# Moving the first head pair's value products behind six more projection steps, and halving the first four loads over two queues

## The chip, the cores and the metric

The kernel runs on one core of a Trainium2 chip. A core has five engines that run their own instruction streams and meet at semaphores: TensorE (PE in the profile; PEld is its weight load), VectorE (DVE), ScalarE (ACT), GpSimd (POOL) and SyncE (SP). SP, ACT and POOL can issue DMA transfers. The metric is the device time of one execution in microseconds, lower is better; times are given as the median of several runs.

## The reference

Two layers of a hybrid encoder over 512 new prompt frames and 8 running streams of 16 frames, 640 frames in all, width 1024, in float32. Cut to what matters here:

```python
x = x + 0.5 * swiglu(rmsnorm(x, g1), w_gu, w_down)          # first feed-forward half step
z = rmsnorm(x, gm) @ w_in                                    # conv B, C, V | q, k, v | gates
s = (q @ k.T) * 64 ** -0.5 + rel_bias[clipped distance]      # 8 heads of 64
s = where(valid chunk band, s, -1e30)
y_attn = softmax(s) @ v
m = sigmoid(g_c) * (y_conv @ w_conv_out) + sigmoid(g_a) * (y_attn @ w_attn_out)
x = x + m @ w_o
x = x + 0.5 * swiglu(rmsnorm(x, g2), w_gu2, w_down2)         # second half step
```

New keys, values and convolution states are outputs too. The first half step begins with the frames `x` and the first weights of `w_gu` in HBM. For the part of the change in the mixer, what counts is that `softmax(s) @ v` of one pair of heads and the projections of the next pairs do not depend on each other.

## The kernel before

**Products.** Every large product is made of three passes of a reduced float32 type: an operand is cut by ACT into `hi` (a cast, line 370) and by DVE into `lo` (the rest, line 376), and PE adds hi·hi, hi·lo and lo·hi in PSUM. Weights come as slabs of 128x1024 from one stream in HBM, cut two slabs ahead of their use. The products of attention itself (scores, transposes, values) are plain float32.

**The opening** (lines 476 to 499 and `opening`, 764 on). Line 479 loads the first half of the frames of `x[0]` with the gains of the first norm (`head`) from SP, line 481 the first 256 columns of weight slab 0 (`raws[0]`) from ACT, line 482 the other half of `x[0]` from SP. The loop at 494 then issues, all from SP, for k = 1 to 7 the block `x[k]` (line 496, 320 KB) and 256 columns of slab 0 or 1 (line 498, 128 KB); line 499 loads the small parameters. `opening` issues a small ACT copy (768, the first ACT work, which loads the activation table), 16 idle products on PE (777), and then for each k the cut of the frames (`plain`, lines 669 to 688), the cut of the weights (`piece`, 785 and 786) and, after each odd k, the 24 products of blocks k-1 and k with both slabs (line 800 for the first 12 of them, 446 for all others). Call blocks 0 and 1 with their weights couple 0, blocks 2 and 3 couple 1.

**The mixer.** In `attention` the order of PE's instructions is the order of the program; ACT, DVE and POOL are ordered by the framework's planner, in which `with soon()` raises a group's priority. A projection of two column tiles (`seven`) is a scheme of seven block products instead of eight. It is cut into 14 steps of six products of 128x320, and `fill(n)` runs the next n steps of the stream of projections. The 14 steps, two at a time, use three PSUM banks: `pa` on X11, `pb` on X21, `pa` on N6, `pc` on T5, `pa` on T7, `pc` on X22, `pa` on T4. Each two are followed by work that reads the bank: the ACT copies of `pa` (line 891), `pa` (899) and `pc` (903), and the DVE additions `first`, `second`, `third` and `last`. A bank is added to further after it was read: the X22 products go on in `pc` after the copy of 903, and the T4 products go on in `pa` after the addition `second` (line 299, `k<-ma_qk,c` in the profile).

For one pair of heads p, `scores(p)` (line 1950) makes the score products into four `att` and two `pr` banks, DVE adds bias and takes maxima (1956), ACT does the exponentials (2150); `turn` transposes the weights on PE (1987) and copies them to SBUF; `values(p)` (2019) makes 16 products into one `att` bank `py`, and ACT copies it to `yas` (2022). Lines 2028 to 2035 give the order for pair 0: `fill(4)`, `turn(0, 0)`, `fill(2)`, `turn(0, 1)`, `fill(2)`, `values(0)`, `fill(6)`, `scores(2)`; for later pairs `values(p)` stands right ahead of `scores(p + 2)`. The six steps behind `values(0)` are, counted from the profile, step 12 (the second X22 step) and steps 13 and 14 (T4) of the projection of q and k of pair 2, and then steps 1 to 3 of that of pair 3. This order is run once in each of the two layers.

Of the kernel before, what the change touches and what calls it, by code (L numbers as in the profile page):

```python
# [16 lines left out]
P = 128  # L17
HP = P // 2
# [5 lines left out]
T = SEQ + NB * TS  # L24
HT = T // 2
# [6 lines left out]
KT = D // P  # L32
# [27 lines left out]
PAD = 64  # L60
# [136 lines left out]
def trunk(ctx: ExitStack, tc: tile.TileContext, xin, wst, small, pbias, samplebias, kcache, vcache, gfin,  # L197
          yout, yrows, ko, vo, co):
    nc = tc.nc
    PE, DVE, ACT, POOL, SP = nc.tensor, nc.vector, nc.scalar, nc.gpsimd, nc.sync  # L200
# [59 lines left out]
    raws, ready = [], []  # L260
# [215 lines left out]
    x = [xp.tile([P, T if k else KT + T], F32, name=f"x{k}") for k in range(KT)]  # L476
    head = x[0][:, :KT]
    m = KT + HT
    SP.dma_start(x[0][:, :m], xin[:, PAD - KT : PAD + HT])
    raws += [wp.tile([P, CH], F32, tag="raw", name=f"raw{i}", bufs=3) for i in range(2)]  # L480
    ACT.dma_start(raws[0][:, : 2 * P], wst[0][:, : 2 * P])
    SP.dma_start(x[0][:, m:], xin[:, PAD + HT : PAD + T])
    x[0] = x[0][:, KT:]
    ident = cp.tile([P, P], F32, name="ident")
    make_identity(nc, ident)
# [7 lines left out]

    for k in range(KT):
        if k:
            SP.dma_start(x[k], xin[:, PAD + k * T : PAD + (k + 1) * T])
            c = slice(k // 2 * 2 * P, (k // 2 + 1) * 2 * P)
            SP.dma_start(raws[k % 2][:, c], wst[k % 2][:, c])
    SP.dma_start(sm, small)
# [903 lines left out]
    def mixer(l, after):  # L1403
        with tc.tile_pool(name=f"yp{l}", bufs=1, reuse_waits="tile") as yp, \
# [18 lines left out]
            with tc.tile_pool(name=f"mp{l}", bufs=2, reuse_waits="tile") as mp:  # L1423
# [62 lines left out]
                with tc.manual_schedule(engines={mybir.EngineType.PE}):  # L1486
                    attention(l, h, st, stats, ops, mp, yas, ycp, both, others())
# [362 lines left out]
    def attention(l, h, norms, stats, ops, mp, yas, ycp, both, others):  # L1850
# [36 lines left out]
        def fill(n):  # L1887
            for _ in range(n):
                next(stream, None)
# [85 lines left out]
        def turn(p, first=None):  # L1975

            if p not in turned:
                turned[p] = [mp.tile([P, offs[-1] + SEQ], F32, name=f"pt{l}_{2 * p + e}", tag="pt")
                             for e in range(2)]
            pt = turned[p]  # L1980

            def blocks(ps, e, js):
                s = weights[2 * p + e]
                n = 0
                for j in js:
                    for i in range(j, NQ):
                        PE.transpose(ps[:, n : n + P], s[:, offs[i] + j * P : offs[i] + (j + 1) * P], ident)
                        n += P

            def take(copy, e, js, ps):  # L1990
                n = sum(width[j] for j in js)
                with soon():
                    copy(pt[e][:, at[js[0]] : at[js[0]] + n], ps[:, :n])

            parts = ((0,), (DVE.tensor_copy,) * 2), ((1, 3), (DVE.tensor_copy, ACT.copy))
            if first is not None:
                parts = (((3, 2), (DVE.tensor_copy, ACT.copy)),) if first else (
                    parts[0], ((1,), (ACT.copy, DVE.tensor_copy)))
            for js, copies in parts:
                for e in range(2):  # L2000
                    ps = (pr if first and not e else att)(f"ptp{l}_{2 * p + e}_{js[0]}")
                    blocks(ps, e, js)
                    take(copies[e], e, js, ps)
            if first is not None:
                return
            ps = pr(f"ptp{l}_{2 * p}_2")
            for e in range(2):
                blocks(ps[:, e * width[2] :], e, (2,))
            for e in range(2):
                take(DVE.tensor_copy, e, (2,), ps[:, e * width[2] :])  # L2010

        def values(p):

            pt = turned.pop(p)
            py = att(f"py{l}_{p}")
            for j in range(NQ):
                for e in range(2):
                    hh = 2 * p + e
                    PE.matmul(py[e * HD : (e + 1) * HD, j * P :], vs[j][:, hh * HD : (hh + 1) * HD],
                              pt[e][:, at[j] : at[j] + width[j]], start=j == 0, stop=j == NQ - 1)  # L2020
            with soon():
                ACT.copy(yas[:, p, 0:SEQ], py)
# [6 lines left out]
        turn(0, 0)  # L2029
        fill(2)  # L2030
        turn(0, 1)
        fill(2)
        values(0)
        fill(6)
        scores(2)
        for p in range(1, npair):
            if p + 1 < npair:
# [487 lines left out]
```

## Time and profile before

| what | us |
|---|---|
| median of 3 runs (lowest to highest) | 2466.82 (2466.36 to 2468.04) |
| the profiled execution's own time | 2465.41 |
| its span, first to last instruction | 2463.6 |
| HBM read over the span | 241.58 MB at a mean of 101 GB/s with what is written |

The page's first part gives each engine's busy time, its share of the span and its instructions; POOL is busy 328.7 us, 13%. In its second part the span stands in 40 slices; the granted TensorE clock is in its highest tenth in all of them. The timeline view gives one line for each instruction or run of like instructions: start in us from the span's start, duration in us, engine (a q behind its name is its sequencer, which issues or waits), line, operation, tiles written and read, shape and count, and in brackets how long the engine was idle before and what ended that. Products on PE overlap, so their pitch is the distance of two starts and not the duration.

### The profile page before, as it was taken

The page shows a single profiled execution, that of the slowest core. Times are in us where ns is not written, and L with a number is a line of the kernel's source. Part 1 is how long each engine was busy: PE and PEld are TensorE (multiplying, and loading weights), DVE is VectorE, ACT ScalarE, POOL GpSimd, SP SyncE. Part 2 cuts the span into 40 slices and gives each one's busy share as a digit, 9 for nine tenths or more (in the row PEclk, how much of TensorE's full clock was granted, in tenths as well). Part 3 has the DMA queues.
Part 4 walks back from the last instruction along what each step waited for, and adds up shares of the span by engine and source line. Part 5 has one row for each costly group of instructions (what it writes and reads, how often), then busy time and mean ns, then how long its engine had stood idle before and what let it go on. Part 6 is the DMA issues. An engine that isn't in the chain of part 4 may idle for free.

```text
span 2463.6 us, 44155 instructions
## 1 busy us (share of the span) xinstructions
PE 2457.2 (100%) x17238; PEld 2409.1 (98%) x17238; DVE 2196.6 (89%) x3729; ACT 1397.6 (57%) x2252; POOL 328.7 (13%) x495
## 2 busy tenths in 40 slices
PE   9999999999999999999999999999999999999999
PEld 9999999889999999999999999998899999999998
DVE  7999999888998899998799999988889989999997
ACT  6555556665655555555665555566656555555555
POOL 0211112211110001011001111121110000111111
PEclk9999999999999999999999999999999999999999
DMA  4543445335443234444334343452444433444444
GB/s 156 143 123 103 117 118 127 112 107 176 119 129 122 87 102 113 108 118 123 107 98 109 109 120 99 118 129 101 140 163 118 123 116 94 108 113 107 113 119 118
DMA packets 115282, 290.93 MB, mean 118 GB/s; under 512 B 13088, under 2 KB 53664, under 8 KB 115072
## 3 DMA queue, kind: packets, MB, share of 16 engines
q1 hardware_dynamic: 69984, 219.96, 26.7%
q0 software_dynamic: 44800, 67.75, 14.6%
q8 instruction: 135, 2.21, 0.4%
q14 instruction: 75, 0.61, 0.1%
q10 hardware_dynamic: 288, 0.39, 0.0%
HBM read 241.58 MB, written 7.94 MB: 101 GB/s over the span
## 4 chain that ended last, share of the span: by engine, by line
PE 100%; ACT 0%; DVE 0%; issue 0%; DVEq 0%; POOL 0%; POOLq 0%
PE pab L470 13%; PE paa L470 11%; PE pcb L470 6%; PE pca L470 6%; PE daa L1204 6%; PE dab L1204 5%; PE po L446 5%; PE qa L470 4%; PE pbb L470 3%; PE pba L470 3%; PE dca L1204 3%; PE dcb L1204 3%; PE ma_cv L470 2%; PE ma_qk L470 2%; PE pv L1903 2%; PE poa L446 2%
## 5 line engine op out<-in xcount | busy, mean ns | idle before, releaser
L370 ACT CAST whi<-raw 128x1024 fp32r<-128x1024 f32 (+1 forms) x564 | 500.5, 892 | 375.8 <-DVE raw L299 63.9
L376 DVE TENSOR_TENSOR wlo<-raw,whi 128x1024 fp32r<-128x1024 f32 (+1 forms) x602 | 580.0, 966 | 136.2 <-ACT whi L370 132.7
L370 ACT CAST whi<-s 128x1024 fp32r<-128x1024 f32 (+1 forms) x166 | 155.3, 935 | 283.4 <-issue 111.2
L470 PE MATMUL pab<-xhib,whi 128*128 128x320 f32 x704 | 217.5, 309 | 0.0
L470 PE MATMUL pab<-xhib,wlo 128*128 128x320 f32 x704 | 217.1, 308 | 0.0
L470 PE MATMUL pab<-xlob,whi 128*128 128x320 f32 x704 | 217.1, 308 | 0.0
L470 PE MATMUL paa<-xhia,wlo 128*128 128x320 f32 x640 | 197.8, 309 | 0.0
L470 PE MATMUL paa<-xhia,whi 128*128 128x320 f32 x640 | 197.7, 309 | 0.0
L470 PE MATMUL paa<-xloa,whi 128*128 128x320 f32 x640 | 197.4, 309 | 0.0
L376 DVE TENSOR_TENSOR wlo<-s,whi 128x1024 fp32r<-128x1024 f32 (+1 forms) x169 | 179.1, 1060 | 3.8 <-ACT whi L370 3.8
L1226 POOL DMA_DIRECT2D x<-c_a x80 | 70.0, 1019 | 569.2 <-ACT ahia L1105 244.8
L1226 POOL DMA_DIRECT2D x<-c_b x72 | 63.0, 1006 | 582.0 <-ACT ahib L1105 205.8
L470 PEld LDWEIGHTS pab<-xhib,whi 128*128 128x128 f32 x704 | 132.2, 188 | 0.9 <-issue 0.9
L470 PEld LDWEIGHTS pab<-xlob,whi 128*128 128x128 f32 x704 | 132.2, 188 | 0.0
L470 PEld LDWEIGHTS pab<-xhib,wlo 128*128 128x128 f32 x704 | 132.1, 188 | 0.0
L470 PEld LDWEIGHTS paa<-xhia,wlo 128*128 128x128 f32 x640 | 120.1, 188 | 0.5 <-DVE wlo L376 0.4
L470 PEld LDWEIGHTS paa<-xhia,whi 128*128 128x128 f32 x640 | 120.1, 188 | 0.5 <-issue 0.4
L470 PEld LDWEIGHTS paa<-xloa,whi 128*128 128x128 f32 x640 | 120.1, 188 | 0.0
L299 DVE TENSOR_TENSOR raw<-s,raw 128x512 f32<-128x512 f32 x166 | 113.1, 682 | 0.0
L470 PE MATMUL pcb<-xhib,wlo 128*128 128x320 f32 x352 | 108.5, 308 | 0.0
L470 PE MATMUL pcb<-xhib,whi 128*128 128x320 f32 x352 | 108.5, 308 | 0.0
L470 PE MATMUL pcb<-xlob,whi 128*128 128x320 f32 x352 | 108.5, 308 | 0.0
(922 smaller groups left out, 8249.1 us busy)
## 6 DMA issues: line engine op xcount, KB each, us to landing
raw<-in_wst SPq DMA_DIRECT2D x374, 512.0 KB, 3.6
x<-c_a POOLq DMA_DIRECT2D x80, 160.0 KB, 4.5
x<-c_b POOLq DMA_DIRECT2D x72, 160.0 KB, 3.6
one<-in_wst POOLq DMA_DIRECT2D x40, 256.0 KB, 3.8
lent<-in_wst POOLq DMA_DIRECT2D x36, 256.0 KB, 4.0
kc<-in_kcache SPq DMA_DIRECT2D x32, 256.0 KB, 4.7
vc<-in_vcache SPq DMA_DIRECT2D x16, 512.0 KB, 4.4
x<-u_a POOLq DMA_DIRECT2D x40, 160.0 KB, 4.3
```

The source lines that it names most:

```text
L299: DVE.tensor_tensor(out=out, in0=a, in1=b, op=op)
L370: ACT.copy(hi[:, d], src[:, c])
L376: DVE.tensor_tensor(out=lo, in0=src, in1=hi.bitcast(F32), op=ALU.subtract)
L446: PE.matmul(ps[:, a, :HT], w, x[a] if isinstance(x, tuple) else x[:, a * HT : (a + 1) * HT], start=first and j == 0 and not seeded, stop=l ...
L470: PE.matmul(ps, a, b, start=start and kp == 0 and j == 0, stop=stop and kp == NP - 1 and j == 2, skip_group_check=True)
L1204: PE.matmul(ps[u], w, y, start=start and i == 0 and j == 0, stop=i == 1 and j == 2, skip_group_check=True)
L1226: POOL.dma_start(x[ms[2 * u + r]][:, cols], z[:, u], accum_op=ALU.add)
L1903: PE.matmul(pv[t], xx[:, t * P : (t + 1) * P], w[:, kk * AW : (kk + 1) * AW], start=c == 0 and kk == 0 and j == 0, stop=c == KT // 2 - 1 a ...
```

## The change

The four first loads (both halves of `x[0]`, the first part of slab 0, and `x[1]`) are each issued as two transfers of 64 partitions, the lower from SP and the upper from ACT. The later loads stay whole and on SP. In `attention`, in both layers, `values(0)` moves from behind the second of eight projection steps to behind all eight, right ahead of `scores(2)`.

```diff
@@ -476,10 +476,16 @@
     head = x[0][:, :KT]
     m = KT + HT
-    SP.dma_start(x[0][:, :m], xin[:, PAD - KT : PAD + HT])
+    def sent(out, src):
+        for q, c in ((SP, slice(0, HP)), (ACT, slice(HP, P))):
+            q.dma_start(out[c], src[c])
+
+    sent(x[0][:, :m], xin[:, PAD - KT : PAD + HT])
     raws += [wp.tile([P, CH], F32, tag="raw", name=f"raw{i}", bufs=3) for i in range(2)]
-    ACT.dma_start(raws[0][:, : 2 * P], wst[0][:, : 2 * P])
-    SP.dma_start(x[0][:, m:], xin[:, PAD + HT : PAD + T])
+    sent(raws[0][:, : 2 * P], wst[0][:, : 2 * P])
+    sent(x[0][:, m:], xin[:, PAD + HT : PAD + T])
...
     for k in range(KT):
         if k:
-            SP.dma_start(x[k], xin[:, PAD + k * T : PAD + (k + 1) * T])
+            (sent if k == 1 else SP.dma_start)(x[k], xin[:, PAD + k * T : PAD + (k + 1) * T])
             c = slice(k // 2 * 2 * P, (k // 2 + 1) * 2 * P)
             SP.dma_start(raws[k % 2][:, c], wst[k % 2][:, c])
@@ -2029,9 +2035,8 @@
         turn(0, 0)
         fill(2)
         turn(0, 1)
-        fill(2)
+        fill(8)
         values(0)
-        fill(6)
         scores(2)
```

## The prediction, made before the changed kernel was timed

> **What bounds the kernel now.** I read the page first, then PE's waits, then the timeline of the two places that the change touches.
>
> ```profile
> span 2463.6 us, 44155 instructions
> PE 2457.2 (100%) x17238; PEld 2409.1 (98%) x17238; DVE 2196.6 (89%) x3729; ACT 1397.6 (57%) x2252; POOL 328.7 (13%) x495
> PE 100%; ACT 0%; DVE 0%; issue 0%; DVEq 0%; POOL 0%; POOLq 0%
> ```
>
> The last line is the chain of work that ended last: it is PE from end to end. PE is busy 2457.2 of 2463.6 us, so its idle time is worth at most 6.4 us, and the whole of PE's listed waiting is this:
>
> ```profile
> PE idle L777 <- POOL epst L491: 1.1, 1, 1.1
> ```
>
> So an edit gains only if PE starts useful products earlier, or spends less time changing from one kind of product to another; it loses as soon as PE has to wait. Both places are looked at with starts, since a busy PE also hides short waits. These are the rows of the opening:
>
> ```profile
> 0.74 0.41 ACTq L481 DMA_DIRECT2D raw<-in_wst  x1
> 0.74 0.39 SPq L479 DMA_DIRECT2D x<-in_xin  x1
> 1.18 1.28 ACT L768 ACT_TABLE_LOAD   x1 [1.18 <-PEq L2497]
> 1.65 0.43 SPq L496 DMA_DIRECT2D x<-in_xin  x1
> 2.12 0.43 SPq L498 DMA_DIRECT2D raw<-in_wst  x1
> 2.47 0.19 ACT L768 COPY early<-epst 128x1 f32<-128x1 f32 x1
> 2.60 0.43 SPq L496 DMA_DIRECT2D x<-in_xin  x1
> 3.92 0.56 ACT L688 ACTIVATE xhia<-x 128x320 fp32r<-128x320 f32 x1 [1.26 <-DMA x<-in_xin]
> 4.39 0.39 ACT L785 CAST whi<-raw 128x256 fp32r<-128x256 f32 x1
> 4.83 0.41 PE L800 MATMUL poa<-xhia,whi 128*128 128x320 f32 x1
> ...
> 7.14 0.33 SPq L496 DMA_DIRECT2D x<-in_xin  x1
> 7.15 0.56 ACT L688 ACTIVATE xhia<-x,x 128x320 fp32r<-128x320 f32 x1 [0.58 <-DMA x<-in_xin]
> 8.36 0.33 SPq L496 DMA_DIRECT2D x<-in_xin  x1
> 8.37 0.83 ACT L675 ACTIVATE xhia<-x,x 128x640 fp32r<-128x640 f32 x1
> 9.23 0.88 DVE L669 SCALAR_TENSOR_TENSOR xloa<-x,x,xhia 128x640 fp32r<-128x640 f32 x1
> 10.17 0.30 PEld L446 LDWEIGHTS poa<-xloa,whi 128*128 128x128 f32 x2 [0.15 <-DVE xloa L669]
> ```
>
> The first real product starts at 4.83, 0.91 after the first operand landed (3.92). From then on PE waits for data once more that counts, 0.15 at 10.17, and the chain to there is the landing of x[2] at 7.15, ACT's cuts up to 9.20, DVE's cut of x[3] from 9.23 to 10.11. Whatever starts PE earlier than 4.83 is waited for again at 10.17, and a later start is free up to about those 0.15 us.
>
> **The change, part one: the halved loads.** Four more transfers are issued: ahead of the first load of slab 1 SP has four (before three), ACT four (before one).
>
> ```profile
> L2068 SPq DMA_DIRECT2D vn<-v x8: 512/518/607, 526.0 to 608.1; - x8
> ```
>
> This is the only transfer of few partitions here, 16 of them, and its issue takes 0.518 us, more than the 0.43 of a whole x load. So a half costs a whole issue: I take 0.47 from the starts 1.65, 2.12, 2.60. ACT then issues at 0.74, 1.18, 1.65 and 2.12 and is free at 2.55 instead of 1.15; its table load (1.28) ends at 3.86 where it ended at 2.46, the small copy (0.19) at about 4.05, and as ACT begins an operation some 0.09 ahead of the end of the one before (3.92 + 0.56 against 4.39), the first cut starts at 3.97 at the earliest, against 3.92. The 1.26 us of idle time ahead of it are the cover, and they are used up. Whether the halves of x[0] land earlier than 3.92 is then of no use. First product: 4.83 + 0.05 = 4.88, inside the 0.15 that PE waits at 10.17 anyway. I count 0.
>
> The other cost is in SP's later issues. Counted in order of issue (slab 0 from ACT, two halves of x[0], x[1], then weights and x in turn), the 6th load is x[2], the 8th x[3], the 14th x[6] and the 16th x[7]. The 14th (7.14) goes out as the 6th lands (ACT takes it at 7.15), the 16th (8.36) as the 8th lands (8.37). So a load waits for the one eight places ahead of it. With four extra transfers, the ninth is now the second slab's first part (2.12 before), and it waits for the first half of x[0]: some 3.5 to 3.9. Everything behind it on SP moves back by the same 1.4 to 1.8 us: x[2] from 2.60 to 4.0 to 4.4. What hides this is the queue's backlog: x[2] lands 4.55 after its issue (2.60 to 7.15), where the first load with nothing ahead of it takes 3.18 (0.74 to 3.92), and the bytes ahead of it stay the same. If the transfers are never starved, x[2] lands at about 7.15 again: 0. With the 3.18 of the unloaded load it would land at 7.2 to 7.6. If nothing of the shift were hidden, PE would wait up to 1.8 longer at 10.17. Ends: -0.5 (x[2] lands earlier by nearly the 0.58 that ACT is idle ahead of it) and +1.8. I take 0: 7.2 is nearest to the row of 7.15, and the 0.15 at 10.17 is there for the rest.
>
> [...]
>
> **Part two: values(0) behind the six steps.** The rows of layer 0, then three of layer 1:
>
> ```profile
> 492.69 0.41 ACT L903 COPY c<-mc_qk 128x320 f32<-128x320 f32 x1
> 492.97 0.31 PE L470 MATMUL ma_qk<-thi,wlo 128*128 128x320 f32 x1
> 492.99 1.06 ACT L370 CAST whi<-raw 128x1024 fp32r<-128x1024 f32 x1
> 493.15 0.41 PE L470 MATMUL mc_qk<-hhim,whi 128*128 128x320 f32 x1
> 493.41 0.31 PE L470 MATMUL mc_qk<-hlom,whi 128*128 128x320 f32 x1
> 493.99 0.31 PE L470 MATMUL mc_qk<-hhim,wlo 128*128 128x320 f32 x1
> 494.08 1.23 DVE L376 TENSOR_TENSOR wlo<-raw,whi 128x1024 fp32r<-128x1024 f32 x1 [1.42 <-ACT whi L370]
> 494.23 2.37 PE L2019 MATMUL py<-pt,v 128*64 128x512 f32 x16
> 495.22 0.48 DVE L299 TENSOR_TENSOR k<-ma_qk,c 128x320 f32<-128x320 f32 x1
> 496.54 0.41 PE L470 MATMUL mc_qk<-hhim,whi 128*128 128x320 f32 x1
> 496.79 0.31 PE L470 MATMUL mc_qk<-hlom,whi 128*128 128x320 f32 x1
> 497.52 0.31 PE L470 MATMUL ma_qk<-thi,whi 128*128 128x320 f32 x1
> 502.01 2.43 PE L1950 MATMUL pss<-k,q 64*128 64x512 f32 x16
> ...
> 1716.06 0.31 PE L470 MATMUL mc_qk<-hhim,wlo 128*128 128x320 f32 x1
> 1717.29 0.49 DVE L299 TENSOR_TENSOR k<-ma_qk,c 128x320 f32<-128x320 f32 x1
> 1719.59 0.31 PE L470 MATMUL ma_qk<-thi,whi 128*128 128x320 f32 x1
> ```
>
> No product is added or taken away. What goes is one change of kind: 493.99 to 494.23 is 0.24 where the pitch inside a step is 0.147 (493.41 to 493.99, four products), so 0.09 is lost going in, and 496.54 to 496.79 is 0.25, so 0.10 is lost coming out. Placed right ahead of the scores the values share their kind:
>
> ```profile
> 520.02 1.46 PE L2019 MATMUL py<-pt,v 128*64 128x384 f32 x11
> 521.41 2.43 PE L1950 MATMUL pss<-k,q 64*128 64x512 f32 x16
> 521.52 0.59 ACT L2022 COPY ya<-py 128x512 f32<-128x512 f32 x1
> ```
>
> That is pair 1, which stands in this order already: the scores take 2.43 there as at 502.01, and the copy of `py` finds ACT free 0.11 after the values end. So the move saves 0.19 a layer, 0.38 in two.
>
> What it takes away is cover. The T4 products of step 13 (497.52) go on in the bank that DVE's addition `second` reads (`k<-ma_qk,c`, 495.22 to 495.70). That addition stands on DVE behind a 1.23 us cut, which itself waited 1.42 for ACT's cast (492.99 to 494.05). Today step 13 comes 1.82 after the addition's end, since the values (2.31, 494.23 to 496.54) lie between. After the move step 12 starts at 493.99 + 0.147 = 494.14, its six products take 0.88, and step 13 is due at 495.02, when the addition has not begun. PE then waits until 495.70 + 0.05. That it does wait is shown by the same kind of place in the same rows: step 11 goes on in `pc`, ACT's copy of `pc` ends at 493.10, and PE's product comes at 493.15, 0.18 after 492.97, with the next one 0.26 behind it. So a released product starts 0.05 after its releaser and costs some 0.11 on the way in. The wait is 495.75 - 495.02 = 0.73, plus 0.11: 0.84 a layer. In layer 1 the addition ends at 1717.78 and step 13 is due at 1716.06 + 0.147 + 0.88 = 1717.09: 0.74 and the same 0.11. Queued behind the waiting product on PE are steps 13 to 17, the values and the scores; nobody else is late, as DVE's and ACT's next work was bound to the old, later times.
>
> Nothing before 493.99 on PE changes and the cast and the cut are in front of it, so I see no reason for DVE to come to that addition sooner; if the planner did put it ahead of the cut, the wait is gone (lower end 0). If it put one more operation ahead, as the 1.23 cut, it is 1.23 worse a layer. I take 0.84.
>
> **Sum.** 2 x (0.84 - 0.19) = +1.3 in the mixers, 0 in the opening: the profiled execution's 2465.41 (span 2463.6 and 1.8 around it) becomes 2466.7. The median of the runs shown, 2466.82, is 1.4 above that execution, so the forecast is 2468.1.
>
> **The rivals.**
>
> *The wait does not come*, because DVE does the addition sooner or PE is not held. For it: the order on DVE is a planner's, and the change gives it another program. Against it: all that decides that order lies before the move. It gives -0.38: 2466.4.
>
> *The eight places decide*, the rival on the slower side. The place is SP's ninth load, at 3.5 to 3.9 instead of 2.12; the price at 10.17 is 0.9, half of the 1.8 of an unhidden shift, on top of the 1.3: 2469.0, and 2469.9 with all of it. It decides if x[2] lands later than about 7.3. For it: the pairs 7.14/7.15 and 8.36/8.37. Against it: a backlog that kept a load 4.55 us on its way.
>
> *The halves pay*: x[0] lands sooner over two queues and ACT, against my count, is ready for it (a half's issue at half the price frees it 0.8 sooner), and x[2] comes up to 0.5 earlier too: 2467.6 with the wait, 2465.9 without it. Against it: the 0.518 of 16 partitions, and the 0.15 at 10.17, which eats any early start alone.
>
> *The change does nothing that it says*: both loads still go over the same transfers, the products are the same, and no PE time moves: 2466.8.
>
> *The planner reorders more than I see*, and several copies in the mixers come late: +4 to +8, 2471 to 2475. For it only that DVE is at 89% of the span.
>
> **How the numbers follow.** Chances: the forecast 0.52, no wait 0.18, eight places 0.12, halves pay 0.09, nothing 0.05, reordering 0.04. The range leaves out the reordering and the lowest corner: it reaches from 2465.6 (the case without the wait less the 0.4 by which a run lies below the median, and the halves' 2465.9) to 2470.2 (2469.0 and the 1.2 by which the highest run lies above the median). A measurement of this kernel can tell about 0.2%, 4.9 us, from no change. All cases but the last are within that, and half of the last is above it: faster 0.01, within 0.96, slower 0.03.
>
> **What would show it.** Right: in both layers a pause of PE ahead of the first T4 product, ended by `k<-ma_qk,c`, of 0.7 or more; no pause between values and scores of pair 0; ACT's table load at about 2.58; SP's fifth issue near 3.5 or later; x[2] taken by ACT at 7.0 to 7.3. Wrong: an addition on DVE ahead of the 128x1024 cut, a first product before 4.7 or after 5.2, a pause at 10.17 that grows above 0.5, or new pauses of PE elsewhere in the mixers.

## The result, and the profile after

| | before | after |
|---|---|---|
| median of 22 runs each | 2466.70 us (2465.86 to 2468.04) | 2469.78 us (2468.81 to 2471.44) |
| ratio of the runs, 95% interval | | 1.0013 (1.0007 to 1.0019) |
| span of the profiled execution | 2463.6 | 2467.8 |

The change costs 3.1 us by the medians and 4.2 us between the two profiled executions. That is 0.13%, below the 0.2% named in the prediction and, with 22 runs, still distinct from nothing. The two sums differ because the profiled execution of before (2465.41) lies 1.3 below its kernel's median and that of after (2469.58) only 0.2 below: 1.1 of the 4.2 belongs to the two executions and not to the change. The page first (its busy times, its chain that ended last), then PE's list of waits after the change:

```profile
PE 2459.2 (100%) x17238; PEld 2410.9 (98%) x17238; DVE 2197.1 (89%) x3729; ACT 1398.2 (57%) x2252; POOL 328.4 (13%) x495
PE 100%; ACTq 0%; ACT 0%; issue 0%; DVE 0%; DVEq 0%
```

```profile
PE ma_qk L470 <- DVE k L299: 1.2, 2, 0.6
PE idle L783 <- POOL epst L497: 1.1, 1, 1.1
PE poa L806 <- ACT whi L791: 0.7, 1, 0.7
```

The page hides what happened: PE is still 100% of the chain and its 17238 products are the same, but its busy time rose by 2.0 us. A product that runs slower counts as busy. The list of waits names two places that were not there before: two waits of `ma_qk` for DVE's `k`, one in each layer, and one wait of the first real product for ACT's cast.

**The opening.** A selection of the timeline's rows after the change (start us, duration us, engine, line, operation, output<-inputs, shapes, count, in brackets the idle time ahead and what ended it):

```profile
0.74 0.56 ACTq L483 DMA_DIRECT2D x<-in_xin  x1
1.33 0.61 ACTq L483 DMA_DIRECT2D raw<-in_wst  x1
1.97 1.26 ACTq L483 DMA_DIRECT2D x<-in_xin  x2
2.25 1.27 SPq L483 DMA_DIRECT2D x<-in_xin  x2
3.26 1.28 ACT L774 ACT_TABLE_LOAD   x1 [3.26 <-issue]
3.56 0.61 SPq L504 DMA_DIRECT2D raw<-in_wst  x1
4.22 0.43 SPq L502 DMA_DIRECT2D x<-in_xin  x1
5.56 0.64 PE L806 MATMUL poa<-xhia,whi 128*128 128x320 f32 x1 [0.66 <-ACT whi L791]
6.62 0.47 PE L806 MATMUL poa<-x2hia,whi 128*128 128x320 f32 x1
6.87 1.02 ACT L681 ACTIVATE xhia<-x,x 128x320 fp32r<-128x320 f32 x2 [0.90 <-DMA x<-in_xin]
6.89 0.47 PE L806 MATMUL poa<-x2hia,wlo 128*128 128x320 f32 x1
8.13 0.56 ACT L694 ACTIVATE xhia<-x,x 128x320 fp32r<-128x320 f32 x1
10.23 0.36 PE L446 MATMUL poa<-x2loa,whi 128*128 128x320 f32 x1
10.43 0.31 PE L446 MATMUL poa<-xhia,wlo 128*128 128x320 f32 x1
```

Three things are to be seen. A half takes ACT 0.56 to 0.63 us to issue, so its four issues end at 3.23, its table load starts at 3.26 (before 1.18) and the first product at 5.56 (before 4.83). Ahead of that product PE pauses 0.66 us. Behind the pause the products come 0.27 apart (6.62, 6.89) where the pitch of before was 0.147, and they keep that pace until 10.2; with 10.43 it is back. Lastly x[1] is taken by ACT at 6.87 and x[2] at 8.13, where before they were there at 5.26 and 7.15. Counted at the 41st real product, a step at which both kernels run at full pace, the opening ends at 13.94 against 11.47: **2.47 us late.**

**The mixer of layer 0**, with the pause of layer 1 as the last two rows:

```profile
495.68 0.42 PE L470 MATMUL mc_qk<-hhim,whi 128*128 128x320 f32 x1
496.61 1.23 DVE L376 TENSOR_TENSOR wlo<-raw,whi 128x1024 fp32r<-128x1024 f32 x1 [1.41 <-ACT whi L370]
497.40 0.31 PE L470 MATMUL mc_qk<-hhim,wlo 128*128 128x320 f32 x1
497.76 0.48 DVE L299 TENSOR_TENSOR k<-ma_qk,c 128x320 f32<-128x320 f32 x1
498.30 0.41 PE L470 MATMUL ma_qk<-thi,whi 128*128 128x320 f32 x1 [0.58 <-DVE k L299]
498.55 0.31 PE L470 MATMUL ma_qk<-tlo,whi 128*128 128x320 f32 x1
502.89 2.38 PE L2025 MATMUL py<-pt,v 128*64 128x512 f32 x16
505.19 0.70 PE L1956 MATMUL pss<-k,q 64*128 64x512 f32 x2
...
1720.13 0.31 PE L470 MATMUL mc_qk<-hhim,wlo 128*128 128x320 f32 x1
1721.03 0.41 PE L470 MATMUL ma_qk<-thi,whi 128*128 128x320 f32 x1 [0.58 <-DVE k L299]
```

The last product of step 12 starts at 497.40 and the next one at 498.30, so 0.75 is lost beside the pitch of 0.147 (the 0.58 in the brackets counts from the end of the product before); the one behind comes 0.25 later, so 0.10 more goes on the restart. From the first product of step 11 to the scores it takes 505.19 - 495.68 = 9.51, against 502.01 - 493.15 = 8.86 before: **0.65 a layer, 1.30 in two.** With 2.47 in the opening, that leaves 0.4 of the 4.2; 0.3 of it lies behind the last product (the last section), the rest is spread thin.

### The profile page after: what moved, and what is told of

Read it like the earlier page. It is cut to its first block, busy times and chain, and to the rows that moved or that the text cites. A ratio compares the mean times of both kernels' runs of the same rounds, so it can differ in the third digit from the quotient of the medians.

```text
span 2467.8 us, 44162 instructions
## 1 busy us (share of the span) xinstructions
PE 2459.2 (100%) x17238; PEld 2410.9 (98%) x17238; DVE 2197.1 (89%) x3729; ACT 1398.2 (57%) x2252; POOL 328.4 (13%) x495
## 4 chain that ended last, share of the span: by engine, by line
PE 100%; ACTq 0%; ACT 0%; issue 0%; DVE 0%; DVEq 0%
PE pab L470 13%; PE paa L470 11%; PE pcb L470 6%; PE pca L470 6%; PE daa L1210 6%; PE dab L1210 5%; PE po L446 5%; PE qa L470 4%; PE pbb L470 3%; PE pba L470 3%; PE dca L1210 3%; PE dcb L1210 3%; PE ma_cv L470 2%; PE ma_qk L470 2%; PE poa L446 2%; PE pv L1909 2%
```

## The experiments

Two theories stood behind the first four. For the opening: the halves' dear issues hold ACT back, the first product is late, and the pause ahead of it costs PE its pace. Its rival: the loads land later, and that alone sets the pace. For the mixers: the wait for DVE's addition. All spans below are those of profiled executions; the 41st product is the mark for the opening, and in before it starts at 11.47. The last column is where the trace's own records of the granted TensorE clock begin; they begin at full, and real products ahead of them come 0.27 apart (6.62 and 6.89 in the changed kernel, 5.44 and 5.71 in two halved).

| run | median, that of before beside it | ratio (95%) | first product, pause ahead | 41st product, behind before | full pace from |
|---|---|---|---|---|---|
| move only | 2467.78, 2466.38 | 1.0006 (0.9997 to 1.0014) | 4.85, none | 11.56, 0.1 | 4.46 |
| halves only | 2468.55, 2466.38 | 1.0010 (1.0001 to 1.0019) | 5.57, 0.66 | 13.81, 2.3 | 9.77 |
| long wake | 2469.05, 2466.38 | 1.0011 (1.0002 to 1.0020) | 5.57, 0.22 | 12.93, 1.5 | 4.31 |
| move, add first | 2466.23, 2466.38 | 1.0000 (0.9991 to 1.0009) | 4.84, none | 11.76, 0.3 | 5.76 |
| two halved | 2469.13, 2466.35 | 1.0012 (1.0003 to 1.0021) | 4.74, none | 13.04, 1.6 | 6.64 |
| halves, one queue | 2472.81, 2466.35 | 1.0025 (1.0014 to 1.0036) | 5.41, 0.52 | 16.89, 5.4 | 4.76; at half again 8.17 to 15.00 |
| short wake | 2467.29, 2466.35 | 1.0003 (0.9995 to 1.0012) | 4.71, 1.51 | 13.19, 1.7 | 10.17 |
| values before 13 | 2466.9 (one run), 2466.35 | | 4.77, none | 12.56, 1.1 | 6.38 |
| column halves | 2468.92, 2466.49 | 1.0009 (1.0000 to 1.0018) | 4.92, none | 13.14, 1.7 | 6.82 |
| x[1] from ACT | 2466.11, 2466.49 | 0.9999 (0.9990 to 1.0008) | 5.08, 0.18 | 11.79, 0.3 | 4.81 |
| both mended | 2466.35, 2466.22 | 1.0000 (0.9991 to 1.0009) | 5.14, 0.25 | 11.97, 0.5 | 6.68 |
| changed, again | 2469.88, 2466.22 | 1.0013 (1.0004 to 1.0022) | 5.57, 0.67 | 14.25, 2.8 | 10.59 |

In before these records begin at 4.73 and in the changed kernel at 10.33.

Five of the intervals lie above 1, but most of them overlap one another, so the verdicts rest on the traces. And one profile is one execution: the very opening of before stands in "move only", "move, add first" and "values before 13", and its 41st product came 0.1, 0.3 and 1.1 late there, the last because x[1] landed 1.1 later (6.33 against 5.23) with nothing changed. A difference in the opening below 1 us needs its rows, not its sum.

### The move alone

```diff
         turn(0, 1)
-        fill(2)
+        fill(8)
         values(0)
-        fill(6)
         scores(2)
```

> Part two alone: the kernel before with the values of pair 0 behind the six steps. Theory (PE waits for DVE's addition before the first product of step 13): +0.65 to +0.70 in each layer, +1.3 to +1.4 in all, so about 2468.1 beside 2466.8; the wait of ma_qk for DVE's k stands in both layers with 1.2 us together, and the opening is the one of before (first product at 4.83). Rival (the whole loss of the changed kernel comes from the opening, and the waits in the mixers are given back later): within 0.3 of before at the end of layer 1's attention. Third: the two parts act on each other, and alone the move costs another sum than +1.37, by more than 0.3.

From the first product of step 11 (493.36) to the scores (502.87) it took 9.51, as in the changed kernel; both waits for `k` stand in the list, 1.2 together; the end came 1.65 later than before, of which 0.2 was there ahead of layer 0's mixer, and the median 1.4. The theory holds, and nothing behind gives it back.

### The halves alone

The loads of the change, in the kernel before (`sent` as defined there):

```diff
-    SP.dma_start(x[0][:, :m], xin[:, PAD - KT : PAD + HT])
+    sent(x[0][:, :m], xin[:, PAD - KT : PAD + HT])
...
-            SP.dma_start(x[k], xin[:, PAD + k * T : PAD + (k + 1) * T])
+            (sent if k == 1 else SP.dma_start)(x[k], xin[:, PAD + k * T : PAD + (k + 1) * T])
```

> Part one alone: the halved loads, with the values of pair 0 at their old place. Theory (the opening's loss stands by itself): first product at 5.56, the idle time ahead of it 0.6 to 0.7, products at a pitch of 0.266 up to about 10.2, and +2.5 from there to the end: about 2469.3. No wait of ma_qk for DVE's k. Rival (the opening's loss is eaten later by slack in the stages behind it): the end within 0.5 of before, 2467.

First product at 5.57, a pause of 0.66, 2.34 late at the 41st product and 2.9 at the end. Move (1.65) and halves (2.9) add up to 4.5, against 4.2 for both; by the medians 1.4 and 2.2 add up to 3.6, against 3.1 and, in the second measurement, 3.7: two separate losses.

### More idle products ahead: no pause, the halves as they are

```diff
-WAKE = 8
+WAKE = 11
```

> The changed kernel with more of the idle products ahead of the first real one (the constant 11 instead of 8, some 22 products instead of 16), so that PE has no pause there. Clock theory (the pause of 0.66 us before the first product is what halves the pace until 10.2): the idle products end near 5.9, the real ones start there at a pitch of 0.147 instead of 0.266, and PE then waits for the cut of x[3], which comes at about 11.4 instead of 10.1: the opening loses 1.3 instead of 2.5, and the end is 1.0 to 1.3 below that of the changed kernel, near 2468.6. Rival (late landings pace the products, the pause is only their first sign): the pitch stays at 0.26 and the time at 2469.8, or 0.3 above it for the later start.

The timeline of PE in this kernel, three rows of its first products:

```profile
6.59 0.31 PE L806 MATMUL poa<-x2hia,wlo 128*128 128x320 f32 x1
6.75 0.33 PE L806 MATMUL poa<-x2loa,whi 128*128 128x320 f32 x1
7.53 0.86 PE L806 MATMUL poa<-xhia,whi 128*128 128x320 f32 x2 [0.45 <-ACT xhia L681]
```

The first product is as late as in the changed kernel, but the pace is full at once (6.59, 6.75) and stays so. The opening loses 1.46 instead of 2.47: between these two executions the half pace was worth 1.0. What is left is the late first product (0.74) and a wait for x[1], not, as I had expected, for x[3]. By the medians it is 2.7 behind before, where the changed kernel was 3.1 and 3.7 behind: 0.4 to 1.0. So the theory of the lost pace holds for some two fifths of the opening's loss in the traces; late operands set the rest. And the 1.0 is not the pause alone: full pace began at 4.31 here, earlier than in any other run, for a reason given behind the next run.

### Fewer idle products ahead: a pause, the loads as before

```diff
-WAKE = 8
+WAKE = 4
```

> The kernel before with half of the idle products (the constant 4 instead of 8), so that PE pauses some 1.9 us ahead of the first real product; no load and no order is changed. Clock theory: the first product stays at 4.83, its successors run at a pitch of 0.266 for some 4.6 us, to about 9.4, where those of before reach 0.147 by 5.8; the opening loses 1.6 to 2.0. Rival (the pace in the opening is set by the landings, and the pause before the first product has no part in it): the pace is that of before, and the opening loses 0 to 0.2.

The timeline of PE in this kernel:

```profile
4.71 0.64 PE L800 MATMUL poa<-xhia,whi 128*128 128x320 f32 x1 [1.51 <-ACT whi L785]
9.28 0.47 PE L446 MATMUL poa<-xhia,wlo 128*128 128x320 f32 x1
10.27 0.46 PE L446 MATMUL poa<-xloa,whi 128*128 128x320 f32 x2
```

The issues are those of before and the first product starts 0.12 earlier, yet the products run 0.27 apart up to 10, and the opening loses 1.7. Nothing but the idle products was changed, so a pause ahead of the first product puts the full pace off: it comes at 10.17, where the four executions with these loads and no pause (before, move only, move with the addition first, values before 13) have it between 4.46 and 6.38. The median rose by 0.9 only, so an ordinary execution may lose less than this profiled one.

The view's column of the granted clock doesn't show it. In the changed kernel it reads 1.00 also in this microsecond, where the products come 0.27 apart (the windows by microsecond; behind the busy times stand the clock, the share of the DMA engines and GB/s):

```profile
8.00:9.00 1.00, 1.00 (x5) 1.00 (x5) 1.00 (x4) 1.00 (x3) 0.00 (x0) 1.00 1.02 314
```

The view counts the clock as full wherever the trace has no record of it, and here the records begin only at 10.33. In an opening the pace has to be read from the starts, or from where the records begin.

These records also say what the pause cost. Their lengths differ by steps of 3.41 us (3.41 and 6.83 with both halves on one queue, 2454.18 in the changed kernel, 2457.60 in before), and the steps fall differently in each execution: PE's idle products start at 1.15 in every run, yet without a pause above 0.25 full pace begins anywhere from 4.31 to 6.82. Counted back from 10.33, the step before runs from 3.51 to 6.92 in the changed kernel, and the pause (4.90 to 5.56) lies in it. From this I estimate that full pace would have come at 6.92 without the pause: it cost one step of 3.4 us at half pace. Counted the same way, a step with 0.25 of idle time still gave full pace (both mended, long wake), one with 0.66 did not; between them nothing was tried. From the first product behind a pause to the full pace it is 4.8 us in the changed kernel (5.56 to 10.33) and 5.5 here (4.71 to 10.17), both between one and two of these steps. Why the pace changes in such steps no run shows.

### Two loads halved instead of four

```diff
-    sent(x[0][:, m:], xin[:, PAD + HT : PAD + T])
+    SP.dma_start(x[0][:, m:], xin[:, PAD + HT : PAD + T])
...
-            (sent if k == 1 else SP.dma_start)(x[k], xin[:, PAD + k * T : PAD + (k + 1) * T])
+            SP.dma_start(x[k], xin[:, PAD + k * T : PAD + (k + 1) * T])
```

> The changed kernel with only the first two loads halved (the first part of x[0] and of the weights); the second part of x[0] and x[1] go whole from SP, so ACT issues two transfers instead of four. Theory (ACT's later issues hold back its table load and with it the first product): ACT's table load at about 1.95 instead of 3.26, the first cut as x[0] lands, 3.5 to 4.1, the first product at 4.4 to 5.0, no pause of PE ahead of it above 0.1 and the full pace from before 7; the opening loses 0.2 to 0.8 instead of 2.5, the mixers still 1.3: some 1.7 to 2.3 below the changed kernel. Rival (the halves themselves are slow on their way, whoever issues them): x[0] and x[1] land as late as in the changed kernel, and the opening still loses 2 or more.

```profile
1.98 1.28 ACT L774 ACT_TABLE_LOAD   x1 [1.98 <-issue]
...
3.85 0.43 SPq L502 DMA_DIRECT2D x<-in_xin  x1
...
5.44 0.47 PE L806 MATMUL poa<-xhia,wlo 128*128 128x320 f32 x1
5.71 0.47 PE L806 MATMUL poa<-x2hia,whi 128*128 128x320 f32 x1
...
8.15 0.56 ACT L694 ACTIVATE xhia<-x,x 128x320 fp32r<-128x320 f32 x1 [0.74 <-DMA x<-in_xin]
```

The first half of what I expected came: table load at 1.98, first product at 4.74, no pause, and full pace before 7. It was not full from the start: the first six products still come 0.27 apart (5.44, 5.71). The second half did not come: the opening still lost 1.6, and my 0.2 to 0.8 was wrong. SP's first three issues (two halves, and the first whole load behind them) took 0.59, 0.82 and 0.60, so x[2] goes out at 3.85 instead of 2.60 and is taken at 8.15 instead of 7.15; from there the cut of x[3] is late, and PE waits 0.35 for it at 11.76. The loss is nearer to the rival's 2 than to mine, but by another cause: no load waited for a place before 8.14, SP simply came to x[2] later.

### Both halves from one queue

```diff
-        for q, c in ((SP, slice(0, HP)), (ACT, slice(HP, P))):
+        for q, c in ((SP, slice(0, HP)), (SP, slice(HP, P))):
```

> The changed kernel with both halves of each of the four loads issued by SP, none by ACT. It tells what makes the issue of a half dear. If it is the shape (64 partitions): SP's issues of the halves keep a pitch of 0.60 to 0.63 with no second queue beside them. If it is two queues issuing at once: they fall to the 0.43 to 0.47 of whole loads. By the theory of ACT's lateness its table load starts near 0.7 to 1.2 and ACT waits for the data again; SP then issues the two halves of the weights third and fourth, at 1.6 to 2.6, and the first product follows their landing, at 5.0 to 5.7, with a pause ahead of it if it is over 5.1.

SP's issues of the halves, four and four:

```profile
0.74 1.23 SPq L483 DMA_DIRECT2D x<-in_xin  x2
2.01 1.24 SPq L483 DMA_DIRECT2D raw<-in_wst  x2
3.29 2.51 SPq L483 DMA_DIRECT2D x<-in_xin  x4
```

Eight halves from 0.74 to 5.80, that is 0.63 each, with no second queue beside them: two queues at once are not what makes an issue dear. ACT is free (its table load starts at 0.73) and waits for data again. All eight on one queue is by far the worst version, as every later load goes out 2.2 later still (x[2] at 6.47 for 4.22). The late loads cost pace as well. PE was at full pace at its first product (the records begin at 4.76), and then waited 0.52, 0.72 and 1.00 for cuts; from 8.17 to 15.00 it was back at half, and here, where the trace has records, the view's column shows it:

```profile
9.01 1.09 PE L806 MATMUL poa<-xhia,whi 128*128 128x320 f32 x2 [1.00 <-ACT xhia L681]
...
11.00:12.00 1.00, 1.00 (x5) 1.00 (x5) 1.00 (x3) 1.00 (x3) 0.00 (x0) 0.50 0.96 285
```

### Halves by columns

```diff
-        for q, c in ((SP, slice(0, HP)), (ACT, slice(HP, P))):
-            q.dma_start(out[c], src[c])
+        w = out.shape[1]
+        for q, c in ((SP, slice(0, w // 2)), (ACT, slice(w // 2, w))):
+            q.dma_start(out[:, c], src[:, c])
```

> The changed kernel with each of the four loads halved by columns instead of partitions: again two transfers over two queues, but each of all 128 partitions and half as wide. Theory (it is the 64 partitions that make an issue dear): the issues fall back to 0.40 to 0.47, ACT's four end at 2.55, its table load starts at 2.55 to 2.65 instead of 3.26, the first cut at 3.95 to 4.1, the first product at 4.85 to 5.05, no pause of PE ahead of it above 0.15. What is left is the lateness of SP's later loads: its fifth issue waits for the first half of x[0], 3.4 to 4.0, x[2] goes out at 4.0 to 4.5 and is taken by ACT at 7.4 to 8.2; the opening loses 0.3 to 1.5 instead of 2.5. Rival (two halves cost as much as in the changed kernel in any shape, as there are eight transfers for four): first product at 5.5, opening 2.3 or more.

```profile
1.65 0.91 SPq L484 DMA_DIRECT2D x<-in_xin  x2
...
2.63 1.28 ACT L775 ACT_TABLE_LOAD   x1 [2.63 <-issue]
3.36 0.33 SPq L505 DMA_DIRECT2D raw<-in_wst  x1
3.74 0.43 SPq L503 DMA_DIRECT2D x<-in_xin  x1
...
8.83 0.56 ACT L695 ACTIVATE xhia<-x,x 128x320 fp32r<-128x320 f32 x1 [1.43 <-DMA x<-in_xin]
```

With all 128 partitions a half costs 0.39 to 0.47, as a whole load does (0.39 to 0.43 for SP's first in before): it is the 64 partitions that are dear. The first product came at 4.92 with no pause. Here the places do decide: SP is free at 2.56 and its fifth issue waits 0.80, to 3.36, for a half of x[0] to land. x[2] goes out at 3.74, earlier than in the changed kernel (4.22), and is taken 0.7 later, at 8.83. So the time of the issue alone does not give the landing; what holds a load on its way for 4 to 5 us I can't tell from these runs.

### x[1] from ACT, nothing halved

```diff
-            SP.dma_start(x[k], xin[:, PAD + k * T : PAD + (k + 1) * T])
+            (ACT if k == 1 else SP).dma_start(x[k], xin[:, PAD + k * T : PAD + (k + 1) * T])
```

> The kernel before with one thing of the change alone: x[1], whole, is issued by ACT behind its weights, so that two queues share the first loads with no half among them. Theory (whole loads cost 0.47 an issue, and ACT has 1.26 us to spare ahead of its first cut): ACT's table load at 1.65, ending 2.93; the first product unchanged, 4.7 to 4.9; every later load of SP goes out 0.47 earlier, x[2] at 2.12, and is taken by ACT at 6.7 to 7.15: the opening is level with before or up to 0.2 ahead of it (PE's wait for x[3]'s cut goes). Rival (a second queue delays what the first one sends): x[0] or x[1] lands later than 3.9 and 5.3, and the opening loses 0.3 or more.

ACT's table load starts at 1.66 and x[2] is taken at 6.99, as the theory has it; but x[0] came at 4.17 instead of 3.92, the first product at 5.08, and the opening is 0.3 behind. Both statements hold in part. The median is level with before (2466.11 against 2466.49): here a second queue that carried whole loads cost nothing and brought nothing that can be measured.

### The move, with the addition ahead of the cut

```diff
...
+        if n.endswith("_qk2"):
+            with tc.issue_after(first_add[0].ins):
+                flush()
         yield from mul(pc, s, 1, X["22"], False)
...
```

`first_add` holds DVE's addition of `second`; the cut left pending by the weights of that step is queued behind it. The values stand behind the six steps as in the changed kernel.

> The kernel before with the values of pair 0 moved, and on DVE the addition that frees the bank (k<-ma_qk) put ahead of the 128x1024 cut that stood before it. Theory (the wait for that addition is the whole cost of the move): no wait of ma_qk for DVE's k, the 0.19 of the changes of kind is saved in each layer, and the end is 0.3 to 0.4 earlier than before: 2466.4, some 1.7 below the move alone. Rival (DVE has no room there: the cut, now 0.5 later, is late for its own products, or ACT's and DVE's later copies are): a new wait of PE for wlo or for k takes the place, 0.3 or more in each layer, and the time is 2467 or more.

Rows behind the scores of layer 0 (DVE's cuts and the softmax, ACT's copy, PE):

```profile
503.84 0.68 DVE L1962 CUSTOM_DVE_ANT_0 yc<-pss,bias 128x512 f32<-128x512 f32 x1
...
508.82 0.40 ACT L901 COPY capsm<-ma_qk 128x320 f32<-128x320 f32 x1
508.90 0.31 PE L472 MATMUL mc_qk<-hhim,wlo 128*128 128x320 f32 x1
509.27 0.41 PE L472 MATMUL ma_qk<-thi,whi 128*128 128x320 f32 x1
```

Up to the scores the theory is right: no wait for `k`, and from step 11 to the scores 502.19 - 493.54 = 8.65, some 0.2 less than before. Then the rival takes it back. DVE's later cuts end at 503.9 instead of 502.9, the softmax begins at 503.84 instead of 503.26, ACT's copy of `capsm` behind it at 508.82 instead of 508.25, and PE's next product in that bank comes 0.37 behind its forerunner instead of 0.147, with 0.10 more on the restart: 0.33 lost, 0.12 a layer worse than before in sum. The median is level with before, and the trace shows that the wait was moved, not removed.

### The values one step later

```diff
-        fill(2)
+        fill(3)
         values(0)
-        fill(6)
+        fill(5)
```

> The kernel before with the values of pair 0 one step later instead of six: behind step 12, ahead of step 13, which is the one that goes on in the bank of DVE's addition. Theory (the move costs only by the cover it takes from that addition): the values still cover it, both changes of kind stay, the end of layer 0's attention and of layer 1's is within 0.1 of before, and no wait of ma_qk for DVE's k stands in the list. Rival (any move of the values behind the planner's place costs, as ACT's copies and DVE's cuts shift): 0.3 or more in a layer.

From the first product of step 11 to the scores 503.21 - 494.36 = 8.85 (before 8.86), no wait for `k` in the list, and the distance to before is 1.2 ahead of layer 0's mixer and 1.2 behind it. The theory holds for this place, the last one ahead of step 13: there the values still cover the addition, and the later place costs nothing.

### Both mended together, and the changed kernel again

"Both mended" is the move with the addition first, and x[1] whole from ACT.

> The two versions that were level with before or ahead of it, put together: x[1] whole from ACT, the values of pair 0 moved, and the addition ahead of the cut on DVE. Theory (neither place costs any more): no wait of ma_qk for DVE's k, no pause ahead of the first product above 0.25, each attention 0.10 to 0.15 slower by its later pause behind the scores, the opening within 0.5 of before: 2466 to 2467, that is within 0.2% of before. Rival (the order on DVE was tuned to the old opening and falls over again): 2468 or more.

> The changed kernel itself once more, unaltered, to see how far its opening repeats: profiles of one and the same opening of before have lain 1.1 apart by the start of a late product. Theory (a late first product and the half pace behind it belong to the change, landings that wander come on top): first product at 5.4 to 5.7 again, a pause of 0.5 to 0.8 ahead of it, the opening 2 to 3 behind before. Rival (the 2.5 was one unlucky execution): an opening less than 1.5 behind, with the first product before 5.2.

The first is level with before (2466.35 against 2466.22), with no wait for `k`, the later pause of 0.33 in both attentions as with the addition first, and the opening 0.5 behind in the trace; no version here beats the kernel before by what can be measured. The second repeats the changed kernel's opening: first product at 5.57, pause 0.67, half pace, 2.8 behind. It was no unlucky execution.

## Why the prediction was right and where it was wrong

The forecast was 2468.1 and the time is 2469.78, inside the range; but 1.3 of the 4.2 us in the traces were foreseen, and most of the rest came from a part that I had counted at 0. That the time lies inside the range is luck: its upper end was set by the rival of the eight places, whose wait for a place did not happen; x[2] was late as that rival has it, but from the dear issues. The miss is 1.7 by the medians and 2.9 by the profiled executions (2466.7 foreseen, 2469.58 measured), since the 1.4 that the sum adds between the two was only 0.2 in the changed kernel. Of the signs that the prediction names, the pauses for `k` in both layers, no pause between values and scores, and SP's fifth issue near 3.5 (3.56) came. The table load and x[2] came later than it says, and the first product, at 5.56, passed the 5.2 that it names as a sign of being wrong. The range's lower end, 2465.6, follows from neither number given for it (2466.4 less 0.4 is 2466.0, and 2465.9); nothing here turns on it.

- **Part two, the mixers: right in mechanism and size.** The wait for `k<-ma_qk,c` ahead of step 13 was put at 0.73 and its restart at 0.11; measured 0.75 and 0.10. The saving of 0.19 shows as some 0.2 in the run where the wait is gone. Net 0.65 a layer, 1.30 in two, as worked out. Where the cover stays (the values ahead of step 13) the loss is nil.
- **"A half costs a whole issue: I take 0.47": the step that failed first.** It measured 0.56 to 0.63 on ACT. The row of 16 partitions (0.518 and more) stood in the prediction and was read as a reason against a cheaper half; it spoke for a dearer one. Four such issues put ACT's table load at 3.26, not 2.58. With the halves that do cost 0.47, the columns, table load, first cut and first product come at 2.63, 4.02 and 4.92, where the prediction's sum has 2.58, 3.97 and 4.88.
- **"The cover, and they are used up", and no price put on running out of it.** A late first product was priced by its lateness alone. It also opens a pause of PE, and the pause puts the full pace off, by an estimated 3.4 us (from the clock records): with the earlier start of the pace in that execution, 1.0 of the 2.5 by the run with the longer row of idle products. In the trace of before sixteen idle products run right up to the first real one; what they are worth was not asked.
- **"x[2] lands at about 7.15 again": wrong by 1.0.** x[2] went out at 4.22, inside the 4.0 to 4.4 foreseen, and was taken at 8.13. The condition was that the transfers are never starved. The same two windows before and then after:

```profile
3.00:4.00 1.00, 1.00 (x6) 1.00 (x6) 0.00 (x0) 0.08 (x1) 0.02 (x1) 1.00 1.08 385
4.00:5.00 1.00, 1.00 (x6) 0.78 (x4) 0.49 (x2) 1.00 (x3) 0.51 (x2) 1.00 1.01 353
```

```profile
3.00:4.00 1.00, 1.00 (x6) 1.00 (x6) 0.00 (x0) 0.74 (x1) 0.35 (x2) 1.00 0.77 222
4.00:5.00 1.00, 0.90 (x5) 0.60 (x3) 0.00 (x0) 0.99 (x3) 0.18 (x1) 1.00 0.91 234
```

  The engines moved 385 and 353 GB/s before and 222 and 234 after. Their busy share fell by less (1.08 and 1.01 to 0.77 and 0.91), so they were short of work, but they also moved fewer bytes in their busy time; why, no run here shows. The only gain was of no use, as the prediction says: both halves of the first part of x[0] had landed at 3.47, where the whole landed at 3.90, and ACT was not free. The loads behind landed later, x[1] at 6.78 for 5.23.
- **The rival of the eight places gave nearly the time (2469.0 to 2469.9), but not by its mechanism.** In the changed kernel the ninth load, SP's fifth, goes out at 3.56, right behind its own issues (2.25 + 1.27 = 3.52), when both halves of x[0] had landed (3.25 and 3.47). Dear issues took the place of the wait. Only with the cheap column halves is the wait seen, 0.80.
- **The two losses in the opening do not add up.** Without the half pace 1.5 is left (long wake); without the late first product 1.6 or 1.7 (two halved, column halves). Either repair alone uncovers the late operands. How much each would be worth in a median, with openings that wander by up to 1 us, these runs can't settle.

## What to carry to other kernels

Cut a load by columns, not by partitions, if it must be cut, and count issue time per transfer from a row of that shape: with few partitions it rose, from 0.43 to 0.6 us. A first product that is late by less than a microsecond can cost more than its lateness, if the pause that it opens falls ahead of the full pace: here full pace came at 10.33, and between 4.31 and 6.82 in the runs without a pause above 0.25. In an opening look at the pitch of the products; the view's clock column reads 1.00 where the trace has no clock record. One execution says little of an opening, as full pace began up to 2.5 us apart in runs without a longer pause. Before work is moved for a cheaper neighbour, ask which wait it covers: 2.3 us of values hid a wait of 0.75, and the saving was 0.2.

## What the runs showed of the hardware beside this

- A transfer of 64 partitions took 0.56 to 0.63 us to issue on ACT and SP, alone or side by side (SP's second took 0.82 or 0.83 in all five runs that have it beside an issue of ACT), one of 128 partitions and half the columns 0.39 to 0.47. The first whole load behind a row of such halves was dear too: 0.61 in the changed kernel (at 3.56), 0.60 with two halved (2.25), 0.58 with one queue (5.84), and only the next fell to 0.43. Halving by partitions over two queues saved no issue time: two issues of 0.6 side by side stood for one of 0.43.
- In all seven executions with halves the end came 0.3 to 0.4 us later behind the last product than in the other seven; in the changed kernel it is 3.81 behind the last issue (2463.99 to 2467.8), in before 3.47 (2460.13 to 2463.6). Nothing in the rows says why, and it wasn't tried.
